# Hybrid decoder block on one core: the weight sums of the down projection placed one set per pair of row blocks, and the down products in another order on two sets of banks

## The chip, the cores and the metric

The kernel runs on one core of one Trainium2 chip. The metric is the device time of one execution in microseconds; the time before is the median of three runs. The profile is of one more execution, whose own time stands in the table below. The numbers after "L" are lines of the kernel before.

## The reference

One decoder layer over 1024 positions and 1024 channels, all in float32: a normed projection feeds two branches side by side (stick-breaking attention with 8 heads, and a gated linear recurrence in chunks), gates merge them, and a dense feed-forward part follows. The change touches the feed-forward part and what stands behind it:

```python
h = x + mixed @ w_out
hn = rms_norm(h, norm2_g)
ffn = (jax.nn.silu(hn @ w_gate) * (hn @ w_up)) @ w_down
return h + ffn
```

w_gate and w_up are 1024 x 2816, w_down is 2816 x 1024. The hidden width of 2816 is 22 row blocks of 128.

## The kernel before

Everything is kept transposed: channels on the partitions, positions along the free axis, in two halves of 512. TensorE takes its operands in a rounded 32-bit format (fp32r). Each float32 operand is therefore split in a high part (a cast, mostly on ScalarE) and a low part (the operand less its high part, a subtraction on VectorE), and each product of two blocks is three matmuls: high by high, high by low, low by high. One matmul is 128 x 128 weights by 128 x 512 columns.

**The feed-forward products are Winograd's seven.** A product of 2 x 2 blocks is made with seven block products in place of eight, from sums of blocks on either side. For gate and up, a pair of row blocks (p and p + 11, so eleven pairs) is one such 2 x 2 problem: `left(src, p, ring)` loads the two weight blocks, makes the sums on VectorE and splits the seven operands; `winograd(a, ring)` issues the seven products in the order 1, 6, 5, 7, 2, 4, 3, each with 4 x 3 matmuls, into three PSUM banks, and reads the banks with adds on VectorE. For every pair there is gate first, then up; the eleven pairs follow one another. The four blocks of silu(gate) * up, and four sums of them, go to DRAM (`act_d`, eight blocks for each pair).

**The sums of the down weights.** Down's left operands need sums of blocks too. `down_sums(p)` (L1056) makes them during the feed-forward part, one set per pair p: two loads of 512 KB of `wd` into two buffers (ring `w2`), four subtractions and additions on VectorE into four buffers (ring `ds`), and four stores of 256 KB to DRAM (`wd_d`). The loads are chained, one after the other (`last_wd`). It is called between gate p and up p in the program's text.

**What sets the order.** Up to the end of the feed-forward part a planner sets it. Each operation is entered with its engine, an estimated duration, the operations whose data it needs, and operations that merely have to be placed before it (`after=`); it takes a slot in a ring of buffers. `Plan.issue` then runs a clock of its own over all of it. When an engine is free, it takes, among the operations whose inputs are there by this clock and whose ring has a free slot, the one of the earliest stage and the highest rank, and among equals the one with the longest way of work behind it. The order that comes out is fixed for each engine's queue. `after=` puts no wait into the program: it sets a place in the order alone. `turn` is the last matmul that was entered, and each product is entered after the one before, so TensorE's order is that of the text. Loads and stores of this part go through SP's queue, but for the stores of `act_d` for the last pair, which ScalarE issues. A queue is worked off in order: what stands behind a waiting instruction waits too. All lines of the planner's instructions read L194 in the profile, so tiles tell them apart.

**The down stage** (from L1112) is written without the planner, and the framework puts its instructions into the queues. Seven products, in the order of `DOWN`, each run over the eleven pairs p: a step loads the left operand (from `wd` or `wd_d`, L1142) and the right one (a block of `act_d`, L1143), 256 KB each on SP's queue, splits both (L247 on ScalarE, L248 on VectorE), and issues 12 matmuls (L1150), three for each of four row blocks d of the output. A product so has 132 matmuls into four banks. The raw and the split operands have six buffers each. The first steps borrow buffers: steps 0 and 1 of product 1 those of the gate weights, step 2 the buffers `w2` (raw) and `ds` (split) of the sums, step 3 `w2` for the raw operands.

Products share banks. Product 1 starts four banks, ScalarE copies them to `acc` (L1176), and the product that goes on in these banks adds to what stands there. Product 6 starts the other four banks. Products that start banks anew are those in `first`, 1, 6 and 5. `finish(o, d)` adds a bank to `hb` (L1158), after products 6, 7 and 4 `acc` as well (L1157), and after products 2, 4, 5 and 3 stores the finished block of the output (L1160). `hb` holds h, 16 blocks of 256 KB, which ScalarE loads back from DRAM (`hb<-h_d`, L1169), two per step. In the last product the last three steps are taken block by block, so that the blocks end one after the other.

Of the kernel before, what the change touches and what calls it, by code (L numbers as in the profile page):

```python
# [15 lines left out]
ALU = mybir.AluOpType  # L16
# [14 lines left out]
BANKS = [3, 2, 3]  # L31
WARM = 9
ORDER = [1, 6, 2, 5, 7, 4, 3]
DOWN = [1, 2, 6, 7, 4, 5, 3]

V_N1, V_N2, V_Q, V_K, V_HG, V_LB = 0, 8, 16, 17, 18, 19
V_W = 27
# [177 lines left out]
def hybrid_block(ctx: ExitStack, tc, xT, wi, wb, wo, wg, wu, wd, vec, outT):  # L215
    nc = tc.nc
# [93 lines left out]
    def hs(h):  # L310
        return slice(h * HALF, (h + 1) * HALF)
# [32 lines left out]
    for n, v in fill_cols[:2]:  # L344
        t = hgp.tile([P, HALF], F32, tag="kb", bufs=4, name="kb")
# [83 lines left out]
    def new(ring, shape=(P, HALF), dt=F32):  # L429
        pool, cap, tag, phase = where[ring]  # L430
        plan.ring(ring, cap)

        def make():
            open_pools(phase)
            return (pools[pool] if phase else pool).tile(list(shape), dt, tag=tag, bufs=cap, name=tag)

        return Buf(ring, make, phase)
# [8 lines left out]
    def V(fn, *args, n=HALF, aps=0, rank=0, part=False, holds=(), after=(), **kw):  # L446
        cycles = 2 * n if fn == nc.vector.tensor_tensor_scan else n
        us = 0.067 + cycles / 960 + 0.061 * aps
        return plan.op("V", us, [(fn, args, kw)], rank, after, part=part, holds=holds)
# [15 lines left out]
    def L(dst, src, kb, rank=0, after=(), part=False, land=None):  # L465
        return plan.op("D", max(0.47, kb / 350), [(nc.sync.dma_start, (dst, src), {})], rank,
                       after, part=part, land=land)
# [5 lines left out]
    act, tt = nc.scalar.activation, nc.vector.tensor_tensor  # L473
# [54 lines left out]
    def take_x(h):  # L528
        ss, acc, ws, sqs = new("ms"), new("tail"), [[], []], []
        if h == 0:  # L530
            plan.ring("kb", 4)
            for u in range(2):
                w = Buf("kb", lambda u=u: first_w[u])
                hi, lo = new("oh", dt=F32R), new("ol", dt=F32R)
                plan.at[A(nc.scalar.copy, hi, w, rank=3)] = 2.4 + 0.6 * u
                V(tt, lo, w, hi.bitcast(F32), op=ALU.subtract, rank=2)
                ws[u].append((hi, lo))
        for k in range(KT):
            x = new("aa" if h == 0 else ("xf", "xq", "xi", "xg")[k // 2])
            load(x, xT[k][:, hs(h)], 256)  # L540
            if h == 0 and k in (2, 3):
                u = k - 2
                n, v = fill[u]
                w = new("kb")
                load(w, wi[COL[n] + v][:, HALF:], 256)
                ws[u].append(split_w(w))
            g = vt[:, V_N1 + k:V_N1 + k + 1]
            A(act, xh[k][h][:, hs(h)], x, AF.Copy, scale=g, aps=1, rank=2 - h)
            V(stt, xl[k][h][:, hs(h)], x, g, xh[k][h][:, hs(h)].bitcast(F32), op0=ALU.mult,
              op1=ALU.subtract, aps=1, rank=2 - h)  # L550
            if k == 0:
                A(act, acc, x, AF.Square, rank=1 - h)
            else:
                sq = new("ww")
                A(act, sq, x, AF.Square, rank=1 - h)
                sqs.append(sq)
        for sq in sqs:
            V(tt, acc, acc, sq, op=ALU.add, rank=1 - h)
        M(2048, [(ss, ones, acc, True, True)])
        rstd(rr[h], ss, D, rank=1 - h)  # L560
        return ws
# [278 lines left out]
    for i, (nm, u) in enumerate(fill):  # L840
        if i == 0:
            ws = take_x(0)
# [5 lines left out]
        elif i > 1:  # L848
            plan.part = "G" if nm == "G" else "s1"
            w = take_w(COL[nm] + u)  # L850
            for h in range(2):
                gate = None
                if nm != "G" and u:
                    d = heads[u - 1]
# [21 lines left out]
    turn = last_fill[0]  # L876
    oo = []
    for k in range(KT):
        t = new("ld", (P, S))
# [18 lines left out]
    for i in range(KT):  # L898
        w = get_w(wb[i])
        ss = []  # L900
        for ring, j in (("s0", i), ("s1", KT + i)):
            t = new(ring, (P, S))
# [24 lines left out]
    for i in range(4):  # L927
# [6 lines left out]
        for e in range(2):  # L934
            k = i + 4 * e
# [120 lines left out]
    def down_sums(p):  # L1056

        ta, tb = new("w2", (P, 1024)), new("w2", (P, 1024))
        for t, r in ((ta, wd[p]), (tb, wd[p + NP])):
            last_wd[0] = L(t, r, 512, after=(last_wd[0],))  # L1060
        a11, a21, a12, a22 = ta[:, :512], ta[:, 512:], tb[:, :512], tb[:, 512:]
        s7, s6, s5, s3 = (new("ds") for _ in range(4))
        V(tt, s7, a11, a21, op=ALU.subtract)
        V(tt, s6, a22, s7, op=ALU.subtract)
        V(tt, s5, s6, a11, op=ALU.add)
        V(tt, s3, a12, s6, op=ALU.subtract)
        for b, t in enumerate((s7, s6, s5, s3)):
            L(wdd[p][:, b * HALF:(b + 1) * HALF], t, 256, part=True)
# [35 lines left out]
    def fb():  # L1104
        return psum2.tile([P, 512], F32, tag="f", name="f")
# [6 lines left out]
    acc1 = [fB.tile([P, HALF], F32, name=f"acc{d}") for d in range(4)]  # L1112
# [7 lines left out]
    TO = {2: [(d, 0) for d in range(4)], 6: [(d, 1) for d in range(4)],  # L1120
          7: [(d + 4, 1) for d in range(4)], 4: [(d + 4, 0) for d in range(4)],
          5: [(d + 4, 1) for d in range(4)], 3: [(d, 1) for d in range(4)]}
    HB = ([(d, 0) for d in range(4)] + [(d, 1) for d in range(8)] + [(d, 0) for d in range(4, 8)])
    LAST = 3
    bank = [None] * 4

    def operands(o, p):

        wp = bp = dB
        tags, btags = ("ah", "al"), ("bh", "bl")  # L1130
        if o == 1 and p < 4:

            rp = wpool if p < 2 else preB
            raw = rp.tile([P, 1024], F32, tag="w", bufs=2, name="w32")
            ra, rb = raw[:, :512], raw[:, 512:]
            if p < 3:
                wp = bp = rp
                tags = btags = ("oh", "ol") if p < 2 else ("ds", "ds")
        else:
            ra = dB.tile([P, HALF], F32, tag="ra", name="ra")  # L1140
            rb = dB.tile([P, HALF], F32, tag="rb", name="rb")
        nc.sync.dma_start(ra, LEFT[o](p))  # L1142
        nc.sync.dma_start(rb, blk(act_d[p], RIGHT[o]))  # L1143
        return split(ra, wp, tags) + split(rb, bp, btags)

    def step(d, p, ops, start):
        hi, lo, bh, bl = ops
        ws = slice(d * P, (d + 1) * P)
        for i, (l, r) in enumerate(((hi, bh), (hi, bl), (lo, bh))):
            nc.tensor.matmul(bank[d], l[:, ws], r, start=start and i == 0,  # L1150
                             stop=p == NP - 1 and i == 2, skip_group_check=True)

    def finish(o, d):
        k, h = TO[o][d]
        t = hb[k][:, hs(h)]
        if o in (6, 7, 4):
            nc.vector.tensor_tensor(t, t, acc1[d], op=ALU.add)  # L1157
        nc.vector.tensor_tensor(t, bank[d], t, op=ALU.add)  # L1158
        if o in (2, 4, 5, 3):
            nc.sync.dma_start(outT[k][:, hs(h)], t)  # L1160

    for o in DOWN:
        first = o in (1, 6, 5)
        final = o == DOWN[-1]
        for p in range(NP - LAST if final else NP):
            ops = operands(o, p)
            if o == 1 and p >= 3:
                for k, h in HB[2 * p - 6:2 * p - 4]:
                    nc.scalar.dma_start(hb[k][:, hs(h)], h_d[k][:, hs(h)])  # L1169
            for d in range(4):  # L1170
                if first and p == 0:
                    bank[d] = fb()
                step(d, p, ops, first and p == 0)
        if o == 1:
            for d in range(4):
                nc.scalar.copy(acc1[d], bank[d])  # L1176
        elif not final:
            for d in range(4):
                finish(o, d)
    rest = [(p, operands(o, p)) for p in range(NP - LAST, NP)]  # L1180
    for d in range(4):
        for p, ops in rest:
            step(d, p, ops, False)
        finish(o, d)


# [25 lines left out]
def build(arrays):  # L1212
    import concourse.bacc as bacc

    nc = bacc.Bacc("TRN2", target_bir_lowering=False, num_devices=1,
                   dynamic_dma_scratch_size=1024)
    args = [nc.dram_tensor(k, v.shape, F32, kind="ExternalInput").ap() for k, v in arrays.items()]
    args.append(nc.dram_tensor("outT", (KT, P, S), F32, kind="ExternalOutput").ap())
    with tile.TileContext(nc) as tc:
        hybrid_block(tc, *args)  # L1220
    return nc
# [11 lines left out]
```

## Time and profile before

| | |
|---|---|
| median of the three runs | 1531.33 us (1530.55 to 1532.29) |
| the profiled execution's own time | 1528.2 us |
| its span, first to last instruction | 1526.5 us |
| TensorE busy | 1502.3 us, 98% of the span, 7213 matmuls |
| VectorE busy | 1196.1 us, 78% |
| ScalarE busy | 804.3 us, 53% |
| first to last store of the weight sums | 886.8 to 1045.2 us |
| first matmul of the down stage | 1308.0 us |
| last matmul of the down stage | 1522.4 us |

A matmul's busy time holds its way through the array, and consecutive matmuls overlap: one takes 0.39 us in the records, and 12 in a row take 2.72 us. So a busy share near 100% doesn't say that matmuls come as closely as they can; how many there are in a stretch of a given length does. Views that are used below: the page's parts; the chain of waits (start, length, what); busy time by stretch; single waits (who waited for whom: total, times, longest); the timeline of an engine (start, length, instruction, and in square brackets the idle time before it and what ended it); and a tile's instructions (duration minimum/median/maximum in ns, first and last start). "PEld" is the loading of weights into TensorE, "SPq" and "ACTq" are the queues of the sequencers that issue DMAs.

### The profile page before, as it was taken

What the parts mean: (1) busy time and instruction counts of PE and PEld (TensorE: products, weight loads), DVE (VectorE), ACT (ScalarE), POOL (GpSimd) and SP (SyncE); (2) the same over time, 40 slices, a digit from 0 to 9 for tenths busy, and PEclk for the clock granted to TensorE, in tenths of its full rate; (3) what the DMA queues carried; (4) which work ended last, traced back from release to release, by engine and by line L of the source; (5) the groups of instructions that cost most, each with busy time, mean ns of one, the idle gap of its engine ahead of it and who ended that gap; (6) DMA issues with size and microseconds to landing.
All of it is one profiled execution on the core that took longest, in us unless ns stands there. A gap on an engine that the chain in (4) does not pass through costs nothing.

```text
span 1526.5 us, 20498 instructions
## 1 busy us (share of the span) xinstructions
PE 1502.3 (98%) x7213; PEld 1240.0 (81%) x7213; DVE 1196.1 (78%) x2092; ACT 804.3 (53%) x1505; POOL 109.2 (7%) x155
## 2 busy tenths in 40 slices
PE   9999999999999999999999998999999999999999
PEld 6778888888888888888888887878888888778887
DVE  9898789988997877967867798998777777475553
ACT  7867778668758877545434452323333333254442
POOL 4210111210111100110000000000000000000000
PEclk9999999999999999999999999999999999999999
DMA  5111111111111111146434357785333333787672
GB/s 183 40 46 56 54 44 40 44 46 61 39 51 52 61 55 62 52 145 216 142 122 155 119 183 236 256 262 172 111 111 112 111 111 109 274 282 222 191 222 92
DMA packets 83159, 188.53 MB, mean 124 GB/s; under 512 B 9584, under 2 KB 11632, under 8 KB 83056
## 3 DMA queue, kind: packets, MB, share of 16 engines
q1 hardware_dynamic: 72400, 167.82, 34.0%
q10 hardware_dynamic: 10656, 19.40, 3.5%
q8 instruction: 57, 0.93, 0.3%
q14 instruction: 46, 0.38, 0.1%
HBM read 131.61 MB, written 55.57 MB: 123 GB/s over the span
## 4 chain that ended last, share of the span: by engine, by line
PE 77%; DVE 12%; DMA 5%; ACT 3%; issue 3%; POOL 1%; SPq 0%; DVEq 0%; ACTq 0%; POOLq 0%
PE pj L194 37%; PE ms L194 17%; PE f L1150 12%; PE z L194 11%; DVE ol L194 2%; DVE aa L194 1%; DMA w<-wu 1%; DMA hb<-h_d 1%; DMA rb<-act_d 1%; DVE g L194 1%; ACT aa L194 1%; DVE kb L194 1%; DVE tail L194 1%; DMA w<-wd 1%; DMA w<-wg 1%
## 5 line engine op out<-in xcount | busy, mean ns | idle before, releaser
L194 PE MATMUL pj<-ah,oh 128*128 128x512 f32 x704 | 286.8, 407 | 2.2 <-ACT tmp L194 0.9
L194 PE MATMUL pj<-al,oh 128*128 128x512 f32 x704 | 275.7, 392 | 0.6 <-DVE al L194 0.5
L194 PE MATMUL pj<-ah,ol 128*128 128x512 f32 x704 | 275.9, 392 | 0.0
L194 ACT CAST oh<-w 128x512 fp32r<-128x512 f32 x164 | 101.1, 621 | 226.2 <-PE z L194 74.1
L194 DVE TENSOR_TENSOR ol<-w,oh 128x512 fp32r<-128x512 f32 x248 | 170.0, 686 | 42.5 <-ACT oh L194 35.6
L194 PE MATMUL ms<-f,oh 128*128 128x512 f32 x528 | 163.8, 392 | 2.3 <-DVE g L194 2.3
L194 PEld LDWEIGHTS pj<-ah,ol 128*128 128x128 f32 x704 | 132.2, 188 | 29.4
L194 PEld LDWEIGHTS pj<-ah,oh 128*128 128x128 f32 x704 | 132.7, 188 | 26.3 <-DVE aa L194 1.5
L194 PEld LDWEIGHTS pj<-al,oh 128*128 128x128 f32 x704 | 132.7, 189 | 25.0 <-DVE al L194 2.5
L194 PEld LDWEIGHTS ms<-f,oh 128*128 128x128 f32 x528 | 99.6, 189 | 24.5 <-DVE g L194 3.5
L1150 PE MATMUL f<-bh,ah 128*128 128x512 f32 x296 | 115.6, 390 | 2.9 <-ACT acc L1176 2.9
L1150 PE MATMUL f<-bl,ah 128*128 128x512 f32 x296 | 115.7, 391 | 0.4 <-DVE bl L248 0.2
L1150 PE MATMUL f<-bh,al 128*128 128x512 f32 x296 | 115.3, 389 | 0.0
L194 DVE TENSOR_TENSOR_SCAN aa<-aa,ww 128x512 f32<-128x512 f32 (+3 forms) x96 | 94.2, 996 | 25.3 <-ACT aa L194 14.6
L248 DVE TENSOR_TENSOR al<-ra,ah 128x512 fp32r<-128x512 f32 x73 | 50.4, 690 | 79.2 <-ACT ah L247 79.2
L194 PE MATMUL z<-f,oh 128*128 128x512 f32 x352 | 110.3, 395 | 1.4 <-ACT oh L194 1.4
L194 PE MATMUL pj<-f,oh 128*128 128x512 f32 x352 | 108.4, 389 | 0.0
L194 PE MATMUL ms<-f,ol 128*128 128x512 f32 x264 | 103.0, 390 | 0.0
L247 ACT CAST ah<-ra 128x512 fp32r<-128x512 f32 x73 | 45.5, 624 | 106.6 <-PE f L1150 92.5
L194 POOL TENSOR_SCALAR oh<-w 128x512 fp32r<-128x512 f32 x84 | 67.2, 800 | 437.6 <-PE pj L194 367.5
L194 PEld LDWEIGHTS z<-f,oh 128*128 128x128 f32 x352 | 66.6, 190 | 16.2 <-ACT oh L194 2.5
L194 PE MATMUL pj<-mx,oh 128*128 128x512 f32 x256 | 78.9, 389 | 0.0
(257 smaller groups left out, 3151.4 us busy)
## 6 DMA issues: line engine op xcount, KB each, us to landing
w<-wi SPq DMA_DIRECT2D x42, 512.0 KB, 3.6
rb<-act_d SPq DMA_DIRECT2D x73, 256.0 KB, 4.3
w<-wg SPq DMA_DIRECT2D x22, 512.0 KB, 3.9
w<-wu SPq DMA_DIRECT2D x22, 512.0 KB, 3.9
w<-wd SPq DMA_DIRECT2D x22, 512.0 KB, 5.7
wd_d<-ds SPq DMA_DIRECT2D x44, 256.0 KB, 5.2
ra<-wd_d SPq DMA_DIRECT2D x44, 256.0 KB, 4.1
act_d<-c SPq DMA_DIRECT2D x40, 256.0 KB, 2.0
```

The lines of the kernel that those rows point to most:

```text
L194: fn(*[a.real() if isinstance(a, View) else a for a in args], **{k: v.real() if isinstance(v, View) else v for k, v in kw.items()})
L247: pin(nc.scalar.copy(hi, src))
L248: pin(nc.vector.tensor_tensor(lo, src, hi.bitcast(F32), op=ALU.subtract))
L1150: nc.tensor.matmul(bank[d], l[:, ws], r, start=start and i == 0, stop=p == NP - 1 and i == 2, skip_group_check=True)
```

## The change

Four edits, all shown in the diff:

- `down_sums`: the first of a set's four sums is entered after `turn`, the last matmul of gate p.
- `DOWN`: the order of down's products becomes 1, 6, 2, 7, 5, 4, 3 in place of 1, 2, 6, 7, 4, 5, 3.
- `SET` and `banks`: the banks are kept as two sets of four. Products 1, 2, 5, 3 use set 0, products 6, 7, 4 set 1, so that each product's set is another than that of the product before it. Product 5 starts set 0 anew, as it took new banks before.
- `HB`: the 16 blocks of h are loaded in steps 0 to 7 of product 6, two per step, in place of steps 3 to 10 of product 1, and in another order of blocks.

```diff
--- before.py
+++ after.py
@@ -31,7 +31,7 @@
 BANKS = [3, 2, 3]
 WARM = 9
 ORDER = [1, 6, 2, 5, 7, 4, 3]
-DOWN = [1, 2, 6, 7, 4, 5, 3]
+DOWN = [1, 6, 2, 7, 5, 4, 3]
 
 V_N1, V_N2, V_Q, V_K, V_HG, V_LB = 0, 8, 16, 17, 18, 19
 V_W = 27
@@ -1060,7 +1060,7 @@
             last_wd[0] = L(t, r, 512, after=(last_wd[0],))
         a11, a21, a12, a22 = ta[:, :512], ta[:, 512:], tb[:, :512], tb[:, 512:]
         s7, s6, s5, s3 = (new("ds") for _ in range(4))
-        V(tt, s7, a11, a21, op=ALU.subtract)
+        V(tt, s7, a11, a21, op=ALU.subtract, after=(turn,))
         V(tt, s6, a22, s7, op=ALU.subtract)
         V(tt, s5, s6, a11, op=ALU.add)
         V(tt, s3, a12, s6, op=ALU.subtract)
@@ -1120,9 +1120,11 @@
     TO = {2: [(d, 0) for d in range(4)], 6: [(d, 1) for d in range(4)],
           7: [(d + 4, 1) for d in range(4)], 4: [(d + 4, 0) for d in range(4)],
           5: [(d + 4, 1) for d in range(4)], 3: [(d, 1) for d in range(4)]}
-    HB = ([(d, 0) for d in range(4)] + [(d, 1) for d in range(8)] + [(d, 0) for d in range(4, 8)])
+    HB = [(d + e, h) for e in (0, 4) for h in (1, 0) for d in range(4)]
     LAST = 3
-    bank = [None] * 4
+
+    SET = {1: 0, 6: 1, 2: 0, 7: 1, 5: 0, 4: 1, 3: 0}
+    banks = [[None] * 4 for _ in range(2)]
 
     def operands(o, p):
 
@@ -1143,11 +1145,11 @@
         nc.sync.dma_start(rb, blk(act_d[p], RIGHT[o]))
         return split(ra, wp, tags) + split(rb, bp, btags)
 
-    def step(d, p, ops, start):
+    def step(o, d, p, ops, start):
         hi, lo, bh, bl = ops
         ws = slice(d * P, (d + 1) * P)
         for i, (l, r) in enumerate(((hi, bh), (hi, bl), (lo, bh))):
-            nc.tensor.matmul(bank[d], l[:, ws], r, start=start and i == 0,
+            nc.tensor.matmul(banks[SET[o]][d], l[:, ws], r, start=start and i == 0,
                              stop=p == NP - 1 and i == 2, skip_group_check=True)
 
     def finish(o, d):
@@ -1155,7 +1157,7 @@
         t = hb[k][:, hs(h)]
         if o in (6, 7, 4):
             nc.vector.tensor_tensor(t, t, acc1[d], op=ALU.add)
-        nc.vector.tensor_tensor(t, bank[d], t, op=ALU.add)
+        nc.vector.tensor_tensor(t, banks[SET[o]][d], t, op=ALU.add)
         if o in (2, 4, 5, 3):
             nc.sync.dma_start(outT[k][:, hs(h)], t)
 
@@ -1164,23 +1166,23 @@
         final = o == DOWN[-1]
         for p in range(NP - LAST if final else NP):
             ops = operands(o, p)
-            if o == 1 and p >= 3:
-                for k, h in HB[2 * p - 6:2 * p - 4]:
+            if o == 6 and p < 8:
+                for k, h in HB[2 * p:2 * p + 2]:
                     nc.scalar.dma_start(hb[k][:, hs(h)], h_d[k][:, hs(h)])
             for d in range(4):
                 if first and p == 0:
-                    bank[d] = fb()
-                step(d, p, ops, first and p == 0)
+                    banks[SET[o]][d] = fb()
+                step(o, d, p, ops, first and p == 0)
         if o == 1:
             for d in range(4):
-                nc.scalar.copy(acc1[d], bank[d])
+                nc.scalar.copy(acc1[d], banks[0][d])
         elif not final:
             for d in range(4):
                 finish(o, d)
     rest = [(p, operands(o, p)) for p in range(NP - LAST, NP)]
     for d in range(4):
         for p, ops in rest:
-            step(d, p, ops, False)
+            step(o, d, p, ops, False)
         finish(o, d)
```

## The prediction

> **What bounds the kernel now.** I read the page's first line, then the chain of waits, then stretches of equal length side by side, and last the single waits.
>
> ```profile
> PE 1502.3 (98%) x7213; PEld 1240.0 (81%) x7213; DVE 1196.1 (78%) x2092; ACT 804.3 (53%) x1505; POOL 109.2 (7%) x155
> ```
>
> ```profile
> 1294.56 2.72 PE z L194 x12
> ...
> 1343.53 179.30 PE f L1150 x789
> 1522.82 0.02 issue
> 1522.85 0.69 DVE hb L1158
> ```
>
> TensorE is the bound almost everywhere. The chain gives its pitch: 12 matmuls in 2.72 us, 0.2267 us each. No matmul is added or removed, so the change can only win back time in which TensorE falls behind that pitch. Stretches of the feed-forward part (two of 162 us) and of the down stage (two of 38 us) show where it does; the columns are window, length, busy time with count for each engine, granted clock, DMA share, GB/s.
>
> ```profile
> 890.00:1052.00 162.00, 154.63 (x658) 124.58 (x657) 144.71 (x237) 50.04 (x85) 0.00 (x0) 0.98 0.73 239
> 1060.00:1222.00 162.00, 162.00 (x716) 134.16 (x715) 128.34 (x207) 51.73 (x87) 0.00 (x0) 1.00 0.32 106
> ...
> 1308.00:1346.00 38.00, 34.67 (x146) 26.66 (x145) 21.73 (x34) 17.19 (x32) 0.00 (x0) 1.00 1.03 364
> 1346.00:1384.00 38.00, 38.00 (x169) 31.44 (x169) 27.42 (x45) 16.52 (x31) 0.00 (x0) 1.00 0.81 259
> ```
>
> The first column in brackets counts matmuls. 658 against 716 is 58 fewer, at 0.2267 us **13.1 us lost** between 890 and 1052. 146 against 169 is 23 fewer, **5.2 us lost** between 1308 and 1346. The second stretch of each pair loses nothing, and 1346 to the end is one unbroken run in the chain. So at most 18.3 us are to be had in the parts that the diff touches.
>
> The lossy stretch is where the sums for down are made:
>
> ```profile
> L194 SPq DMA_DIRECT2D wd_d<-ds x44: 319/423/1062, 886.8 to 1045.2; - x44
> L194 DVE TENSOR_TENSOR ds<-w,ds x22: 678/682/693, 887.3 to 1044.5; 128x512 f32<-128x512 f32 x22
> ```
>
> All 44 stores go out between 886.8 and 1045.2, eleven sets at 14.4 us each, while eleven pairs of row blocks take 14 products of 2.72 us each, 38.1 us a pair. The waits from 890 to 1052 say how this reaches TensorE:
>
> ```profile
> PE z L194 <- DVE ol L194: 3.9, 4, 1.9
> PE ms L194 <- DVE g L194: 2.1, 2, 1.3
> PE z L194 <- ACT oh L194: 1.4, 2, 1.2
> ...
> SPq L194 <- DVE ds L194: 54.5, 34, 10.7
> ...
> DVE ds L194 <- DMA w<-wd: 6.6, 5, 1.9
> ```
>
> VectorE waits in its order for down's weights, SP waits in its order for VectorE's sums with the next gate and up weights queued behind, and the split of a weight, or the read that frees a bank, comes late.
>
> **The change part by part.**
>
> *Pacing (the first sum of a set may not be placed before its gate's last product).* The same 44 sums, 22 loads and 44 stores are issued; only their place on VectorE and on SP's queue moves. A set costs VectorE 4 instructions, 2.4 us at their start-to-start of 0.60 us (932.33 to 932.92 below). The cover is VectorE's idle time in the stretch without sums: 162 - 128.34 = 33.7 us over 162 / 38.1 = 4.25 pairs, 7.9 us a pair.
>
> ```profile
> 932.33 0.68 DVE L194 TENSOR_TENSOR ds<-w,ds 128x512 f32<-128x512 f32 x1
> 932.92 0.68 DVE L194 TENSOR_TENSOR g<-g,rr 128x512 f32<-128x512 f32 x1
> ...
> 1256.75 0.68 DVE L194 TENSOR_TENSOR c<-ms,p 128x512 f32<-128x512 f32 x1
> 1257.35 0.68 DVE L194 TENSOR_TENSOR ol<-w,oh 128x512 fp32r<-128x512 f32 x1
> 1259.66 0.69 DVE L194 TENSOR_TENSOR ol<-w,oh 128x512 fp32r<-128x512 f32 x1 [1.63 <-ACT oh L194]
> 1261.96 0.69 DVE L194 TENSOR_TENSOR c<-ms,p 128x512 f32<-128x512 f32 x1 [1.60 <-PE ms L194]
> ```
>
> 2.4 fits 7.9 three times. The planner gives free VectorE slots to the operation with the longest way behind it, and a sum has little behind it, so it fills holes such as the two of 1.6 us shown. A hole taken wrongly costs its successor 0.6 us at most; the add at 1256.75 is over at 1257.43 and its bank is written again one product after the z product that starts at 1256.32 below, at 1259.04, so 1.6 us are spare.
>
> ```profile
> 1256.32 0.62 PE L194 MATMUL z<-f,oh 128*128 128x512 f32 x2
> ```
>
> The next set's weights are loaded when the set before lets go of its two buffers, some 35 us before use, so that VectorE's wait for w<-wd goes. The trace doesn't show paced sums: their gain lies between 0 (each set stalls as now) and 13.1. I take 12.5, nearer the stretch without loss, keeping 0.6 for a late split here and there.
>
> Part of the 13.1 is clock, in the two stretches with 0.91:
>
> ```profile
> 940.00:960.00 20.00, 17.97 (x72) 0.91 0.69 210
> 1020.00:1040.00 20.00, 18.27 (x73) 0.91 0.60 196
> 1320.00:1340.00 20.00, 19.24 (x80) 1.00 1.05 386
> ```
>
> 9% of 20 us is 1.8 us, twice: 3.6 us. They follow waits at once (the two rows below: a wait of 1.88 us, then double pitch), so I let them go with the waits.
>
> ```profile
> 943.75 0.50 PE L194 MATMUL z<-f,ol 128*128 128x512 f32 x1 [1.88 <-DVE ol L194]
> ...
> 945.67 1.06 PE L194 MATMUL z<-f,oh 128*128 128x512 f32 x2
> ```
>
> The Trainium skill (TensorE: Matmul & The Clock Gate, Part 1: The HAM clock gate) says that the half rate comes back after an idle window of about 3.4 us; by that a wait of 1.88 us would not explain it. The trace doesn't agree: double pitch stands 2 us behind this wait, and none stands behind the longer one of 2.88 us below. What hangs on that rule is a rival below.
>
> *Two sets of banks in turn.* Product 1 now ends in banks that product 2 continues, and ScalarE must copy them first:
>
> ```profile
> 1339.26 0.39 PE L1150 MATMUL f<-bh,al 128*128 128x512 f32 x1
> 1342.53 0.50 PE L1150 MATMUL f<-bh,ah 128*128 128x512 f32 x1 [2.88 <-ACT acc L1176]
> ...
> 1340.86 0.61 ACT L247 CAST bh<-rb 128x512 fp32r<-128x512 f32 x1
> 1341.38 0.61 ACT L247 CAST ah<-ra 128x512 fp32r<-128x512 f32 x1
> 1341.90 0.57 ACT L1176 COPY acc<-f 128x512 f32<-128x512 f32 x1
> ```
>
> 1342.53 - 1339.26 - 0.2267 = 3.04 us, with 0.3 more at the next banks. In the new order product 6 starts on the other set; the copies have its 132 matmuls, 29.9 us, as cover. Every later neighbour pair (6-2, 2-7, 7-5, 5-4, 4-3) changes set too, and the adds that drain a product have a whole product to run in. Where the old order continued a bank at once (6-7, 7-4, 5-3) the unbroken run shows that it cost nothing, so nothing is gained there. Gain 3.3 us; after the last product the same add and store remain.
>
> *h in the second product.* The other 1.9 of the 5.2 us lie from 1320 to 1340, where DMA carries 386 GB/s: two operand loads and two loads of h per step of 12 matmuls (4 x 262,144 bytes in 2.72 us are 385 GB/s). The splits of an operand pair come every (1336.12 - 1326.94) / 3 = 3.06 us there, against a step of 2.72:
>
> ```profile
> 1326.94 0.68 DVE L248 TENSOR_TENSOR bl<-rb,bh 128x512 fp32r<-128x512 f32 x1
> ...
> 1336.12 0.68 DVE L248 TENSOR_TENSOR bl<-rb,bh 128x512 fp32r<-128x512 f32 x1
> ```
>
> ```profile
> L1169 ACTq DMA_DIRECT2D hb<-h_d x16: 326/327/503, 1308.0 to 1337.8; - x16
> ```
>
> Without h product 1 needs 193 GB/s, so from step 4 on the loads run ahead into six buffers each of raw and split operands. When the 16 loads of h come in steps 0 to 7 of product 6, the rate is the same 386, eight steps fall behind by 8 x 0.34 = 2.7 us, and one step of lead covers that. Between 0 (covered) and 2.7 us (no lead) I take 0.4 for pitch under full DMA. ScalarE issues these loads, 16 x 0.33 us, and they stand in its order among the splits, now product 6's instead of product 1's; from 1346 to 1384 it is busy for 16.52 of 38 us, which covers 5.2. The adds of product 6 are the first to need h: its four blocks come with steps 0 and 1, nine steps or 24 us before the add. By the 358 GB/s per core that the Trainium skill (DMA: Bandwidth & Descriptors, Specifications) gives, the 8.39 MB of those steps would need 23.4 us, not 21.8, and without lead the sum would be 1.6 us worse; the trace's 386 is above that figure.
>
> *What the pacing makes late.* Product 1's third step puts its splits into the four buffers of the sums (ds), its raw operands into w2:
>
> ```profile
> L1150 PE MATMUL f<-ds x12: 389/389/390, 1313.4 to 1315.9; 128*128 128x512 f32 x12
> ...
> L247 ACT CAST ds<-w x2: 609/616/622, 1047.3 to 1047.9; 128x512 fp32r<-128x512 f32 x2
> ```
>
> Now they are ready at 1047, 266 us early. Paced, the last set comes after the last gate, about 1289, its sums fill holes until about 1299, its stores land up to 5 us later; splits at 1304 to 1307 meet a need at 1313.4. If ScalarE's order has them behind the last stores of the activations, they start at 1312.75:
>
> ```profile
> 1310.37 2.38 ACTq L194 DMA_DIRECT2D act_d<-bs  x4
> ```
>
> Two casts and two subtractions then end at about 1314.7, one step late by 1.1 us. Between 0 and 1.1 I take 0.2.
>
> **Sum.** 12.5 + 3.3 + 1.9 - 0.4 - 0.2 = 17.1 us. The profiled execution took 1528.2 us, 1.7 more than its span of 1526.5; so 1511.1 in its terms. The median of the runs, 1531.33, lies 3.1 above it: **1514.2 us**.
>
> **The rivals.**
>
> *Each set costs what it costs now* (13.1 / 11 = 1.2 us), because four stores held in SP's order delay the weights behind them however far the sets are apart. For it: the 54.5 us of SP's waits. Against: the holes, and weights loaded long before. Then 3.3 + 1.9 - 0.6 = 4.6 us: 1526.7; half of it, 1520.5.
>
> *h binds in product 6*, no lead: 2.7 instead of 0.4, 1516.5.
>
> *The clock dips are not the waits' doing* and stay: 1514.2 + 3.6 = 1517.8. For it: the wait of 2.88 us without a dip. Against: both dips stand right behind a wait. The rule cited above from the Trainium skill (TensorE: Matmul & The Clock Gate, Part 1) would have it so.
>
> *Slower: SP holds the weights.* Every set's four stores wait in SP's order for sums at the end of VectorE's preference; the next weights wait behind. The splits lead: counted in the order of the products, the one at 1257.35 serves the ms product at 1264.64 below, 6.6 us after its end. The longest wait of SP for a sum is 10.7 us; each set then costs 4.1 us, 45 us in all: about 1559. It decides from 6.6 + 17.1 / 11 = 8.2 us of hold on. Against: with weights landed, four sums in 7.9 us of holes.
>
> ```profile
> 1264.64 2.72 PE ms L194 x12
> ```
>
> *It doesn't do what it says*: the planner's clock runs apart from the chip's, or sums bunch at another place, and the loss moves with them: within 3 us of 1531.
>
> **How the numbers follow.** Forecast (1512 to 1518) 75%; each set costs as now, wholly or half, 9%; h binds 4%; clock 3%; slower 5%; no effect 4%. The range reaches from all 18.3 us won, with 2 us for the spread of the runs, 1511, to most of the half-way case, 1522.5. About 0.2%, 3 us, can be told from no change: faster 0.91, within 0.04, slower 0.05.
>
> **What would show it.** Right: stores wd_d<-ds spread from about 895 to 1290, some 38 us between sets; no PE wait for DVE ol or DVE g after 895; clock 1.00 throughout; no ACT acc wait; 16 loads of h after 1320 without a wait at product 6; ds splits before 1310. Wrong: 640 to 680 matmuls in any 162 us of the feed-forward part, SP waits for DVE ds near 8 us, or a gap before the third step of product 1.

## The result and the profile after

The changed kernel takes **1520.4 us** (median of 4 runs, 1518.5 to 1520.8); the kernel before, run beside it, takes 1531.8. The ratio is 0.9922, with a 95% interval from 0.9905 to 0.9939. That is 11.4 us faster and 6.2 us short of the forecast of 1514.2: inside the wide range of 1511 to 1522.5, but outside the 1512 to 1518 that the prediction gave 75%.

The profiled execution of the changed kernel took 1520.8 us, its span is 1519.1. In views of this and the other runs the numbers after "L" are lines of that run's own kernel: L1152 and L1154 are there what L1150 is in the kernel before (the matmuls of down), L1171 what L1169 is (the loads of h), L1178 what L1176 is (the copies to `acc`). Here are the stretches that the prediction set side by side, now of the changed kernel (window, length, busy time with count of PE, PEld, DVE, ACT and POOL, granted clock, DMA share, GB/s):

```profile
890.00:1052.00 162.00, 159.36 (x694) 129.40 (x695) 133.00 (x217) 52.03 (x88) 0.00 (x0) 1.00 0.49 159
1060.00:1222.00 162.00, 161.69 (x702) 130.45 (x701) 133.77 (x219) 48.09 (x82) 0.00 (x0) 1.00 0.51 166
...
1305.00:1343.00 38.00, 38.00 (x170) 31.33 (x169) 20.17 (x31) 15.38 (x26) 0.00 (x0) 1.00 0.95 325
```

A full stretch of 162 us holds 716 matmuls. 694 are 22 fewer: 5.0 us lost at 0.2267 us each, where 13.1 were lost before. 702 are 14 fewer: 3.2 us lost where nothing was lost before. The start of the down stage holds 170 matmuls and loses nothing. In the same window the kernel before holds 148, 5.0 us fewer:

```profile
1305.00:1343.00 38.00, 34.72 (x148) 27.17 (x148) 20.12 (x31) 14.19 (x26) 0.00 (x0) 1.00 0.96 336
```

So the down stage gave all it could, while the pacing thinned the loss in the feed-forward part and spread it over every pair of row blocks. The granted clock is 1.00.

The chain of waits of the changed kernel, cut to one pair (start, length, what), shows what sets the pace in such a pair:

```profile
1212.44 0.68 DVE g L194
1213.73 0.61 DVE ol L194
1214.38 2.56 PE z L194 x10
1216.95 2.88 PE ms L194 x12
1219.85 0.69 DVE c L194
1221.17 5.06 DMA w<-wu
1226.86 0.68 DVE c L194
...
1236.71 4.36 DMA w<-wg
```

TensorE is no longer the whole chain. Eight times from 890 to 1300 the chain passes through a load of an up weight, 5.0 to 6.6 us long (5.06 in this pair), and through VectorE behind it. A load of a gate weight stands in it too; the experiments below leave that load alone, and the loss goes all the same. VectorE's timeline at that place (start, length, operation, and in brackets the idle time before it and what ended it) shows how:

```profile
1222.57 0.69 DVE L194 TENSOR_TENSOR c<-pj,g 128x512 f32<-128x512 f32 x1
1226.25 0.69 DVE L194 TENSOR_TENSOR w<-w 128x512 f32<-128x512 f32 x1 [2.99 <-DMA w<-wu]
1226.86 0.68 DVE L194 TENSOR_TENSOR c<-ms,p 128x512 f32<-128x512 f32 x1
```

VectorE's order holds the first subtraction on an up weight (`left`) ahead of the add that drains a bank (`c<-ms,p`), so VectorE stands for 2.99 us and all that follows is late. TensorE meets the delay twice: at the gate's product 7, which needs a bank that VectorE has to read first, and at the next up's product 5, which needs a low part that VectorE has to make. The waits from 890 to 1300 of the changed kernel, TensorE's and the largest of VectorE:

```profile
PE ms L194 <- DVE g L194: 2.7, 4, 1.6
PE z L194 <- DVE ol L194: 0.7, 3, 0.3
...
DVE w L194 <- DMA w<-wu: 30.6, 10, 4.6
```

The view lists only the longer of TensorE's waits; the rest are 0.05 to 0.5 us each, with about 0.1 at the next matmul. And the load is slow because of its place on SP's queue (SP's timeline, start, length of issue, operation):

```profile
1216.16 0.33 SPq L194 DMA_DIRECT2D w<-wd  x1
1216.55 0.42 SPq L194 DMA_DIRECT2D wd_d<-ds  x1
1217.97 0.33 SPq L194 DMA_DIRECT2D w<-wd  x1
1218.35 0.51 SPq L194 DMA_DIRECT2D wd_d<-ds  x1
1221.17 0.33 SPq L194 DMA_DIRECT2D w<-wu  x1
```

The last sums of a set let go of their weights, and the two loads of the next set go out at once, 1 MB just ahead of the up weight. The up weight, issued at 1221.17, has landed at 1226.25; the planner's constants (1.46 us of issue and 2.0 of landing, `FROM`) put VectorE's use 3.46 us behind the issue. On the chip VectorE stands there from 1223.26 on, 2.1 us behind the issue.

### The profile page after: what moved, and what is told of

Read it like the earlier page. It is cut to its first block, busy times and chain, and to the rows that moved or that the text cites. A ratio compares the mean times of both kernels' runs of the same rounds, so it can differ in the third digit from the quotient of the medians.

```text
span 1519.1 us, 20504 instructions
## 1 busy us (share of the span) xinstructions
PE 1501.8 (99%) x7213; PEld 1238.3 (82%) x7213; DVE 1194.1 (79%) x2092; ACT 804.3 (53%) x1505; POOL 110.3 (7%) x155
## 4 chain that ended last, share of the span: by engine, by line
PE 69%; DVE 18%; DMA 5%; ACT 4%; issue 3%; POOL 1%; SPq 0%; DVEq 0%; ACTq 0%; POOLq 0%
PE pj L194 34%; PE f L1152 14%; PE ms L194 13%; PE z L194 8%; DVE ol L194 4%; DMA w<-wu 3%; DVE g L194 3%; DMA w<-wg 2%; DVE w L194 2%; DVE c L194 1%; DVE aa L194 1%; ACT aa L194 1%; ACT oh L194 1%; DVE kb L194 1%; DVE bs L194 1%
## 5 line engine op out<-in xcount | busy, mean ns | idle before, releaser
L194 PEld LDWEIGHTS pj<-ah,ol 128*128 128x128 f32 x704 | 132.6, 188 | 29.8
L1152 PE MATMUL f<-bh,ah 128*128 128x512 f32 x296 | 115.2, 389 | 0.0
L1152 PE MATMUL f<-bh,al 128*128 128x512 f32 x296 | 115.2, 389 | 0.0
L1152 PE MATMUL f<-bl,ah 128*128 128x512 f32 x296 | 115.1, 389 | 0.0
L194 PEld LDWEIGHTS pj<-f,oh 128*128 128x128 f32 x352 | 66.1, 188 | 13.7
```

The source lines that it names most:

```text
L194: fn(*[a.real() if isinstance(a, View) else a for a in args], **{k: v.real() if isinstance(v, View) else v for k, v in kw.items()})
L1152: nc.tensor.matmul(banks[SET[o]][d], l[:, ws], r, start=start and i == 0, stop=p == NP - 1 and i == 2, skip_group_check=True)
```

## The experiments

Three theories stood at first. **A**: VectorE stands in its order because the use of the up weight is planned too close behind its load. **B**: the sums stand where VectorE has no room, whatever the weights do. **C**: the load itself is late behind down's loads. All ratios are to the kernel before, run beside each; matmuls are counted in the two windows of 162 us above, in one execution each. The three runs with the landing of 3.6 us and the pacing have the same program up to the end of the feed-forward part and hold 707, 711 and 702 in the first window, so a difference of some ten matmuls, 2 us, says little by itself.

| run | median us | ratio (95%) | matmuls 890-1052, 1060-1222 |
|---|---|---|---|
| the change | 1520.4 | 0.9922 (0.9905-0.9939) | 694, 702 |
| down stage alone | 1524.2 | 0.9945 (0.9933-0.9957) | 665, 717 |
| pacing alone | 1527.2 | 0.9968 (0.9955-0.9980) | 706, 696 |
| landing 3.6 us | 1512.3 | 0.9871 (0.9857-0.9884) | 707, 716 |
| sums in up | 1524.6 | 0.9948 (0.9934-0.9961) | 712, 697 |
| landing, unpaced | 1528.1 | 0.9974 (0.9965-0.9983) | 652, 711 |
| down's loads behind up's | 1511.1 | 0.9864 (0.9850-0.9877) | 714, 716 |
| landing, h in product 1 | 1515.8 | 0.9894 (0.9880-0.9907) | 711, 716 |
| landing, old order, h second | 1521.7 | 0.9934 (0.9921-0.9947) | 702, 710 |
| landing, and down's loads behind up's | 1511.2 | 0.9860 (0.9844-0.9877) | 715, 717 |
| sums in up but the last | 1517.8 | 0.9903 (0.9888-0.9919) | 710, 698 |
| paced by the loads alone | 1512.6 | 0.9867 (0.9852-0.9882) | 715, 716 |

**The two halves of the change.** Down stage alone (against the changed kernel):

```
-        V(tt, s7, a11, a21, op=ALU.subtract, after=(turn,))
+        V(tt, s7, a11, a21, op=ALU.subtract)
```

> The changed kernel without its pacing: the sums for down are placed as before, the down stage is the new one. The two profiles lose 4.9 us (before) and 0.0 us (after) from 1327 to 1345, so the down stage alone should be worth 4.9 us, my prediction said 4.6: 1531.8 - 4.9 = 1526.9 us, 1525.5 to 1528.5. If the pacing gave all that lies between the medians except this, 11.45 - 4.9 = 6.5 us, the other half shows in the run with pacing alone. Rival: the down stage gives more than its own waits, because loads of its first product no longer meet late stores of the sums: under 1524.

Measured: 1524.2 us, a gain of 7.6, more than the 4.9 of the single waits that the profile of before shows (5.0 by the count above). The rival was that loads in product 1 meet fewer late stores, but the last store of a sum goes out at 1045.2 in the kernel before and at 1043.9 in this run, long before. The next run shows where the rest comes from. Pacing alone (against the kernel before):

```
-        V(tt, s7, a11, a21, op=ALU.subtract)
+        V(tt, s7, a11, a21, op=ALU.subtract, after=(turn,))
```

> The kernel before with the pacing alone: down's order, banks and loads of h stay as they were. If the parts add up: 1520.4 + 4.9 = 1525.3 us, TensorE losing some 9.5 us spread from 939 to 1276 and 4.9 us from 1327 to 1345. If the pacing is worth only the 3.5 us by which the two profiles differ in the sums' stretch (13.0 - 9.5): about 1528.3. If it is worth nothing by itself: 1531.

Measured: 1527.2 us, a gain of 4.7. 7.6 + 4.7 = 12.3 against 11.4 for both: the parts add up, within the intervals. The old down stage in this run has the same wait for ScalarE's copies as before, and something behind it that the profile of before has not (TensorE's timeline, idle time before it in brackets):

```profile
1336.47 0.39 PE L1150 MATMUL f<-bh,al 128*128 128x512 f32 x1
1339.86 0.80 PE L1150 MATMUL f<-bh,ah 128*128 128x512 f32 x1 [3.00 <-ACT acc L1176]
1340.46 0.63 PE L1150 MATMUL f<-bl,ah 128*128 128x512 f32 x1
1340.88 0.63 PE L1150 MATMUL f<-bh,al 128*128 128x512 f32 x1
```

From 1339.86 to 1346.0 the matmuls start 0.43 us apart instead of 0.2267, about 14 of them: 2.8 us more. In the profile of before a wait of 2.88 us at this place had no such run behind it. With it the old down stage costs 4.9 + 2.8 = 7.7 us, which is what the first run gained. That the timed runs of the kernel before mostly have it is an inference from that match, for they leave no trace. Their granted clock is on record, though, and supports it: 0.9977 on average in the nine runs of the kernel before, 0.9984 in the five with the pacing alone, 0.9990 in the five with the down stage alone, 1.000 in the four of the change. In the profile here a clock of 0.998 goes with the 2.8 us; by that, an estimate, the clock makes some 1.8 of the 7.6 us, and 0.9 stay open.

**Where the rest of the pacing's gain stays.** The landing, against the changed kernel:

```
-                last_wu[0] = L(t, r, 512, after=(last_wu[0],))
+                last_wu[0] = L(t, r, 512, after=(last_wu[0],), land=3.6)
```

> The changed kernel with one number of its planner different: a load of an up weight is taken to land 3.6 us after its issue slot instead of 2.0, so that VectorE's order has other work where it now stands 2.99 us (1226.25) for the second up weight of a pair. The sums keep their place. Theory A (VectorE stands in its order for a weight that is planned too early, and carries the delay to the gate's product 7 and on to the next up's product 5): both losses of a pair go, 5.2 + 4.3 = 9.5 us, 1511 to 1513. Theory B (the sums stand where VectorE is busiest, from the gate's end to up's product 7, and cost there whatever the weights do): the gate's 5.2 us may go, up's 4.3 stay, 1515 to 1517. Theory C (the load itself is late behind the loads of down's weights and the stores of the sums): the wait moves with it, 1518.5 to 1521.

Measured: 1512.3 us, 8.1 better than the change, by one number in the planner and no change in what the chip executes except its order. Theory A's range holds it, B's and C's do not. VectorE's timeline of this run at the same place:

```profile
1215.73 0.69 DVE L194 TENSOR_TENSOR c<-pj,g 128x512 f32<-128x512 f32 x1
1218.45 0.69 DVE L194 TENSOR_TENSOR c<-ms,p 128x512 f32<-128x512 f32 x1 [2.03 <-PE ms L194]
1219.18 0.69 DVE L194 TENSOR_TENSOR c<-c,g 128x512 f32<-128x512 f32 x1
1219.79 0.69 DVE L194 TENSOR_TENSOR w<-w 128x512 f32<-128x512 f32 x1
```

The draining add now stands ahead of the weight's subtraction and runs when its bank is ready. The up weight is as late as before (issued at 1214.33, 4.9 us to landing), and nobody waits for it.

Down's loads behind up's, against the changed kernel:

```
-            last_wd[0] = L(t, r, 512, after=(last_wd[0],))
+            last_wd[0] = L(t, r, 512, after=(last_wd[0], last_wu[0]))
```

> The changed kernel (1520.4 us) with the loads of down's weights held on SP until up's weights are issued; the planner's landing stays 2.0 us. In the changed kernel the up load issued at 1221.17 lands 5.1 us later, behind two loads of down's weights and two stores of sums; loads that stand alone land in 3.5 us. Theory C (that crowding is the cause): VectorE's stand of 2.99 us falls to about 1.4 and the losses of a pair at least by half: 1513 to 1516. Theory A (VectorE's order puts the use too close behind the load, whatever else is on the queues): little changes, 1518 to 1522. The run with the landing of 3.6 us speaks for A: its up load, issued at 1214.33, still takes 4.9 us and nobody waits for it.

Measured: 1511.1 us, 9.3 better than the change. I had expected little; theory C holds too, and better than its own range. The answer of the trace on its DMA issues from 1213 to 1215 (tile, count, size, median us to landing), and VectorE's timeline:

```profile
w<-wd SPq DMA_DIRECT2D x2, 512.0 KB, 5.8
w<-wu SPq DMA_DIRECT2D x1, 512.0 KB, 3.5
```

```profile
1214.85 0.69 DVE L194 TENSOR_TENSOR c<-pj,g 128x512 f32<-128x512 f32 x1
1216.92 0.69 DVE L194 TENSOR_TENSOR w<-w 128x512 f32<-128x512 f32 x1 [1.38 <-DMA w<-wu]
1217.57 0.69 DVE L194 TENSOR_TENSOR c<-ms,p 128x512 f32<-128x512 f32 x1
```

VectorE's order is the old one and it still stands for the weight, but for 1.38 us, as C had said, because the load lands in 3.5 us instead of 5.1. The Trainium skill (DMA: Bandwidth & Descriptors, Queues, rings and completion order) says that SP's transfers share one row of rings, whose descriptors are consumed in ring order; the pair of runs agrees, with 5.1 us behind the two loads and 3.5 ahead of them. Over all pairs from 890 to 1300 VectorE stands for up weights 16.0 us in ten waits, where it was 30.6 in ten in the changed kernel:

```profile
DVE w L194 <- DMA w<-wu: 16.0, 10, 2.3
```

These waits cost next to nothing: the chain of waits of this run from 1160 to 1300, by line, is TensorE alone:

```profile
by line: PE ms L194 41.1%; PE z L194 29.1%; PE pj L194 27.2%; PE f L1152 2.6%
```

So A and C name two factors of one delay. VectorE can stand for 1.6 us in a pair, the mean here, and make it up; at 3.1, the mean of the changed kernel, it cannot, and either remedy brings it below that point. Down's loads behind up's is also the version to keep: 1511.1 against 1531.5 us, faster than both kernels. Both edits together:

> Both remedies at once: landing of up's weights planned at 3.6 us, and down's weights loaded behind up's. If they mend one and the same delay (VectorE standing for an up weight that lands behind down's loads), nothing is left to add to the better of them, 1511.1 us: 1510.5 to 1512. If each mends a delay of its own, the 1.5 us that TensorE still loses from 890 to 1300 with the landing alone go too, but not below 1510. If they are in each other's way (the later place of VectorE's use meets the later loads of down): 1513 or more.

Measured: 1511.2 us, the same as the better one alone: one and the same delay.

**Where the sums stand.** After up's product 4 instead of after the gate:

```
         prod(y, a, 4, False)
+        mid[0] = turn
...
-        V(tt, s7, a11, a21, op=ALU.subtract, after=(turn,))
+        V(tt, s7, a11, a21, op=ALU.subtract, after=(mid[0],))
```

with `down_sums(p)` called behind up's `winograd`.

> The changed kernel with the sums placed after up's product 4 instead of after the gate's last product: into the part of a pair where VectorE is idle between its adds (1218 to 1226 in the changed kernel). Theory A alone, if the weight is still planned 3.46 us after its load: VectorE stands as long, the gate's 5.2 us stay, 1515 to 1517. Theory B: the sums leave the busiest place, up's splits come in time, the two loads of up's weights go out together again as in the kernel before from 1060 on (2.7 us apart, not 8.8 and 30), and the loss goes: 1511 to 1513. Rival: the sums now stand ahead of the next gate's first adds and cost there: above 1520.

Measured: 1524.6 us, by two losses. In five pairs TensorE waits at up's product 7 for an add of VectorE (0.48 us at 1252.98 in its timeline, and some 0.3 more at that matmul and the next). TensorE's waits from 890 to 1300:

```profile
PE ms L194 <- DVE c L194: 2.4, 5, 0.5
```

VectorE has no wait for an up weight left, but a smaller loss stands in place of the old one. Over the two windows together this run holds 1409 matmuls and the next one 1408, against 1396 and 1402 in the change and in the run with the pacing alone, which have the sums at the gate's end: this place is at most 1.4 to 2.9 us better. And down's product 1 waits at its third step (TensorE, then ScalarE):

```profile
1307.32 0.39 PE L1154 MATMUL f<-oh,ol 128*128 128x512 f32 x1
1313.86 4.63 PE L1154 MATMUL f<-ds 128*128 128x512 f32 x10 [6.15 <-ACT ds L247]
```

```profile
1306.95 4.99 ACTq L194 DMA_DIRECT2D act_d<-bs  x4
1311.98 0.62 ACT L247 CAST ds<-w 128x512 fp32r<-128x512 f32 x1 [20.16 <-DMA act_d<-bs]
```

That is the lateness which the prediction priced at 0 to 1.1 us and took as 0.2: the last set's sums run so late that ScalarE's order has the splits into their buffers behind the stores of the last activations. With the last set alone put back behind its gate:

```
+        else:
+            mid[0] = turn
+            down_sums(p)
         x, c = winograd(au, "c")
-        down_sums(p)
+        if p + 1 < NP:
+            down_sums(p)
```

> The run with the sums after up's product 4 (1524.6 us), with the last set alone put back behind the last gate, as in the changed kernel. That run lost 6.31 us and about 2.4 us of double pitch behind it at the third step of down's product 1, where TensorE waited for ScalarE's split in a buffer of the sums (ds). If the last set, 14 us later there, is the cause: 1524.6 - 8.7 = 1515.9, 1515 to 1517, and what is left is 0.65 us per pair at up's product 7. If ScalarE's stores of the activations or the raw loads are the cause: the wait stays, 1522 to 1525.

Measured: 1517.8 us; no wait of TensorE is left from 1300 to 1346. The last set's place was the cause. The time is 1.9 us above the expectation: without the lateness 8.7 us should have gone, and 6.8 went. It is 2.6 us below the change, but the two intervals overlap.

**Is the pacing needed?** The sums' wait for the gate taken out, first of the run with the landing, then of the run with down's loads behind up's:

```
-        V(tt, s7, a11, a21, op=ALU.subtract, after=(turn,))
+        V(tt, s7, a11, a21, op=ALU.subtract)
```

> The run with the landing of 3.6 us (1512.3 us), with the pacing taken out: sums placed as before, new down stage. It differs from the run with the down stage alone (1524.2 us) in the landing only. If the landing of up's weights is the whole story, the pacing is not needed: 1512 to 1514. If unpaced sums lose by waits of their own (VectorE's order standing for down's weights, eleven sets in 158 us on SP's queue), the landing mends little there: 1521 to 1525, and the pacing is worth 9 to 12 us once VectorE's order has the right landing, against 4.7 alone.

Measured: 1528.1 us, 3.9 worse than the down stage alone and outside both expectations. The trace shows where: VectorE's waits for up weights are gone (3.6 us in 3 with the down stage alone), but it now stands for down's weights twice as long, 14.7 us against 7.0 in 7 waits:

```profile
DVE ds L194 <- DMA w<-wd: 14.7, 13, 1.9
```

The two windows hold 19 matmuls fewer than with the down stage alone, 4.3 us. That these waits are the whole cause was not tested. With the landing, pacing is worth 1528.1 - 1512.3 = 15.8 us; without it, on the same down stage, 1524.2 - 1520.4 = 3.8. With down's loads behind up's:

> The run with down's weights behind up's (1511.1 us), without the wait of the sums for the gate: only the loads are paced, one set per pair, and the planner puts the sums where it likes (in its order some 15 us after the gate's end). If pacing the loads is what counts, because it keeps the next set's two loads away from the front of up's second weight: 1510 to 1513. If the place of the sums counts as well: as the sums in up's tail cost 0.65 us per pair at product 7 there, 1516 or more.

Measured: 1512.6 us, and 715 and 716 matmuls in the two windows. The stores of the sums are spread from 888.2 to 1262.4. Its interval overlaps those of the three other best runs. So what counts is one set of loads per pair, kept behind up's loads; the place of the sums then follows from them.

**The down stage's two edits**, both on the run with the landing. h back in product 1:

```
-            if o == 6 and p < 8:
-                for k, h in HB[2 * p:2 * p + 2]:
+            if o == 1 and p >= 3:
+                for k, h in HB[2 * p - 6:2 * p - 4]:
```

> The run with the landing of 3.6 us (1512.3 us), with the 16 loads of h put back into product 1; down's order and its two sets of banks stay new. The old place lost 1.9 us from 1320 to 1338 by waits for the splits of operand pairs. If that place is the cause: 1514.2, with waits of TensorE for bl in product 1. In the changed kernel the 16 loads of h still go out from 1305 to 1341, while product 1 runs, one per step instead of two: if only the halved rate matters, the waits come back all the same with two per step, and the price is again 1.9; if neither, 1512.3 within 1 us, and the 1.9 us came from what else stood on the queues.

Measured: 1515.8 us, 3.5 more than with h in product 6 (2.3 between the two profiled executions), and the waits for low parts are back (TensorE's waits from 1300 to 1346):

```profile
PE f L1152 <- DVE bl L248: 0.9, 3, 0.3
```

The place of h in the text decides, then, though the loads hardly moved: in the changed kernel they go out while product 1 runs, thinned out rather than put off:

```profile
L1171 ACTq DMA_DIRECT2D hb<-h_d x16: 326/327/584, 1305.7 to 1346.3; - x16
```

16 loads in 40.6 us, where before had 16 in 29.8 (1308.0 to 1337.8). The two runs compared here have 39.3 (1297.1 to 1336.4, h in product 6) and 30.0 (1297.0 to 1327.0, h in product 1). ScalarE's order runs ahead of TensorE by the buffers of the operands, and takes the loads with it.

The old order of products on one set of banks, with h in its second product:

```
-DOWN = [1, 6, 2, 7, 5, 4, 3]
+DOWN = [1, 2, 6, 7, 4, 5, 3]
...
-    SET = {1: 0, 6: 1, 2: 0, 7: 1, 5: 0, 4: 1, 3: 0}
+    SET = {1: 0, 2: 0, 6: 0, 7: 0, 4: 0, 5: 0, 3: 0}
...
-            if o == 6 and p < 8:
+            if o == 2 and p < 8:
```

> The run with the landing of 3.6 us (1512.3 us), with down's products in their old order on one set of banks (product 2 continues the banks of product 1) and the loads of h in the second product of that order. If the wait for ScalarE's copies is worth what the trace of before shows, 3.04 + 0.3 us: 1515.6. In the run with the pacing alone the same wait of 3.17 us was followed by 6 us of matmuls at double pitch, 2.8 us more, which the profile of before does not have: then up to 1518.4. The waits for bl in product 1 should be gone here as well, or else h is not their cause.

Measured: 1521.7 us, 9.4 more, beyond the 3.3 to 6.1 expected. The waits for bl are gone, but the wait for the copies has grown (TensorE, then ScalarE):

```profile
1330.47 0.39 PE L1152 MATMUL f<-bh,al 128*128 128x512 f32 x1
1336.43 0.80 PE L1152 MATMUL f<-bh,ah 128*128 128x512 f32 x1 [5.57 <-ACT acc L1178]
1337.02 0.63 PE L1152 MATMUL f<-bl,ah 128*128 128x512 f32 x1
```

```profile
1328.11 4.73 ACTq L1171 DMA_DIRECT2D hb<-h_d  x3
1332.96 0.62 ACT L247 CAST ah<-ra 128x512 fp32r<-128x512 f32 x1 [4.24 <-DMA hb<-h_d]
...
1335.80 1.07 ACT L1178 COPY acc<-f 128x512 f32<-128x512 f32 x2
```

The profile shows 5.7 us at this wait and about 2.9 in the 14 matmuls at double pitch behind it, 8.6 of the 9.4; the profiled execution is the slowest of the five, 1524.4, and loses 2.5 more in the feed-forward windows, where this run's program is that of the run with the landing. ScalarE stands 4.24 us in the issue of h's loads, ahead of the copies in its order. On two sets of banks nobody waits for these copies; on one, TensorE does. Without the second set moving h gains nothing: the down stage loses 8.6 us here, and 7.7 in the run with the pacing alone, which has h in product 1.

## Why the prediction was right, and where it was wrong

The direction and the mechanism by parts were right, the sizes were not, and that the time came inside the wide range is partly luck: by the runs alone the pacing gave 4.7 of its 12.5 us, 7.8 too little, and the down stage 7.6 where 4.6 were forecast, 3.0 too much. In terms of the profiled execution it is the offset, last in this list, that covered part of the error.

- **Pacing, 12.5 us: wrong size.** Between the two profiles it won 13.1 - 5.0 - 3.2 = 4.9 us in the two windows; by the runs 4.7 alone, and 3.8 on the new down stage. The step that failed is the one on the loads: "the next set's weights are loaded when the set before lets go of its two buffers, some 35 us before use, so that VectorE's wait for w<-wd goes". That wait went, but the sentence asked only when the loads are wanted and not what stands behind them on the queue: the up weight, which VectorE's order wants 3.46 us after its issue by the plan and 2.1 on the chip. The argument on holes (2.4 us into 7.9) fell with it: idle time on average does not help an engine that stands in order for 3 us just before it is needed. With the loads put behind up's, the windows hold 714 and 716 matmuls, 0.5 us lost: the 12.5 us are there, in another version (1524.2 - 1511.1 = 13.1 us against the down stage alone).
- **The rival "each set costs what it costs now or half"** gave 1520.5 for the half, and 1520.4 was measured, but its reason was not the cause. SP waits as long for the sums in the changed kernel (174.9 us from 890 to 1300 in 43 waits, the longest 14.5) as in the run with down's loads behind up's, which loses nothing to it. SP's waits of that run, the longest row:

```profile
SPq L194 <- DVE ds L194: 174.9, 44, 14.3
```

- **Slower, SP holds the weights:** holds of 14.5 us came, well over the 8.2 from which it was to decide; the run with down's loads behind up's has them too (14.3) and loses next to nothing. The weight behind them has to wait for its buffer anyway: the up weight goes out at 1221.17, just behind the end of a split of VectorE (1220.46 and 0.68 us) that frees it.
- **The down stage, 3.3 + 1.9 - 0.4 - 0.2 = 4.6:** its 5.0 us of loss are wholly gone in the profile, so the two deductions were 0. In the runs it is worth 7.6; most of the rest is, by the inference above, double pitch behind the bank wait, which the one execution that I read does not have. Some 0.5 of the 1.9 us from 1320 to 1340 belonged to the bank wait already, for the matmul that waited was due at 1339.49. That h would run in product 6's steps was wrong; it runs thinner, over products 1 and 6.
- **What the pacing makes late:** right for this change. The splits into the sums' buffers ran before 1310, as named (one line of the changed kernel: count, durations, first and last start), and the term of 0.2 us was 0. The run with the sums in up shows the price when the cover is gone: 6.15 us of wait and 2.4 of double pitch, where I had put 1.1 as the worst.

```profile
L247 ACT CAST ds<-w x2: 622/622/623, 1294.7 to 1296.3; 128x512 fp32r<-128x512 f32 x2
```

- **Clock:** the dips went with the long waits, as forecast. That they follow such waits at once was wrong, as the last section shows.
- **The offset of 3.1 us** between the profiled execution and the median was carried over as if it belonged to the measurement. For the changed kernel it is -0.4 (1520.8 and 1520.4). Why the one execution of the kernel before was faster than its timed runs stays open: its granted clock, 0.997, lies among theirs (0.996 to 0.999). In profiled terms the forecast was 1511.1 against 1520.8, 9.7 us too good; the offset took 3.5 of that back.

Of the signs named, spread stores, clock and no wait for acc came as said; PE waits for DVE ol and g after 895, and 694 and 702 matmuls, told of the pacing's shortfall. The loads of h did not wait until 1320 (1305.7 to 1346.3).

## What to carry to other kernels

When a buffer is freed earlier or later, ask what its refill will stand in front of on the queue, and compare the planner's landing with the longest landing in the trace there, not with that of a lone load. An engine that runs in order needs its loads to have landed with room to spare; here stands of 1.6 us a pair cost next to nothing, and stands of 3.1 cost some 9 us over eleven pairs. A forecast from one profiled execution should count the spread between that execution and the timed runs as part of what it does not know, and not carry it over as a constant: it was 3.1 us before and -0.4 after.

## What the hardware showed unexpectedly

The granted clock does not follow from the length of a wait. The profile of before has a wait of 1.88 us at 943.75 with double pitch 2 us behind it. The run with the down stage alone has the same wait at the same place, and the normal pitch behind it (TensorE's timeline):

```profile
943.77 0.50 PE L194 MATMUL z<-f,ol 128*128 128x512 f32 x1 [1.88 <-DVE ol L194]
...
945.28 0.39 PE L194 MATMUL z<-f,ol 128*128 128x512 f32 x1
945.51 0.62 PE L194 MATMUL z<-f,oh 128*128 128x512 f32 x2
```

At the wait for acc it was 2.88 us without and 3.00 us with; the waits of 5.57 and 6.15 us both had it. So in these traces a wait of 2 to 3 us may or may not bring double pitch, which then costs some 1.8 to 2.9 us. One program shows both: the five timed runs of the down stage alone have granted clocks from 0.998 to 1.000. The Trainium skill (TensorE: Matmul & The Clock Gate, Part 1: The HAM clock gate) says that the gate watches a window that runs freely, so that the moment of a change depends on where in the window the work falls; that agrees with the same wait having both outcomes. Its figure of about 3.4 us of idleness does not agree with 1.88 and 3.00 us being enough.
